# A row normalisation on one core: a second load that waits for a ScalarE write, and a last-store wait moved between two exit-barrier instructions

## The chip, the core and the metric

The kernel runs on one core of one Trainium2 chip. A core has a matrix engine (TensorE, PE, unused here), VectorE (DVE), ScalarE (ACT), GpSimd (POOL) and SyncE (SP). Each engine runs its own list of instructions in order, and semaphores order the engines against each other. Transfers between HBM and the on-chip memory are issued by an engine (here always SP) and then carried out by 16 DMA engines, which this text calls lanes. Each lane adds one to the transfer's semaphore when its share has landed, so a transfer is complete at 16.

The metric is device time in microseconds of one execution. Smaller is better.

## The reference

```python
def setup_inputs():
    batch, dim = 1024, 4096
    return {"x": np.random.randn(batch, dim).astype(np.float32),
            "axis": -1, "eps": np.float32(1e-12)}

def reference(x, axis, eps):
    norm = np.sqrt(np.sum(x ** 2, axis=axis, keepdims=True) + eps)
    return (x / norm).astype(np.float32)
```

Each of 1024 rows of 4096 float32 values is divided by its own Euclidean norm. 16.78 MB are read and 16.78 MB written.

## The kernel before

The 1024 rows are spread over 128 partitions, 8 rows to a partition, and handled in two tiles of 4 rows per partition (R = 4, n_tiles = 2). A tile is `xt`, 128 partitions by 4 x 4096 floats, 8.39 MB, and each tile has a buffer of its own. There are four transfers in all: two loads (L219) and two stores (L240), each of a whole tile, each issued by SP on its one queue. A partition's share of a tile is contiguous, 64 KB, and is one packet of a lane, so a lane moves eight packets per transfer.

For each row of a tile the work is: the sum of squares (on ACT, L33, for rows 0, 1 and 2; on DVE, L42, for row 3), the norm (ACT square root, L53, then the DVE reciprocal, L59), and the scaling in place (DVE, L64). Row 2 of the first tile is scaled by both engines, 3584 columns on ACT (L72) and 512 on DVE (L78); row 2 of the second tile is scaled on DVE alone. Then the tile is stored. The small results are `ssq` (sums of squares) and `rstd` (reciprocal norms), one column per row of the tile. `eps_t` is a 128x1 tile that DVE fills at the start (L211).

The Python program writes this down in the order of the loop at L224, but the framework's scheduler decides the order of each engine's list from what it thinks is ready. In the program as built, ACT's list in the first tile is: squares of row 0, norm of row 3, norm of row 0, squares of row 1, norm of row 1, squares of row 2, norm of row 2, scaling of row 2 (its part). In the second tile it is: squares of row 0, norm of row 0, squares of row 1, norms of rows 3 and 1, squares of row 2, norm of row 2. DVE scales in the order in which the norms come: rows 3, 0, 1, 2 in the first tile and 0, 3, 1, 2 in the second. ACT needs one table of functions for squares (loaded at the start, L33) and another for square roots (loaded before the first norm, L53).

Two functions edit the finished program by hand. `first_load_to_front` moves the first load ahead of the entry barrier, so that it is SP's first instruction; the second load follows the entry barrier. `gpsimd_waits_for_last_store` edits the end. The program ends in two barriers over the five engines. In each, the other four engines signal their arrival, GpSimd takes the four arrivals in one instruction and releases the others in the next. The function removes from SP the wait for the last store's semaphore and gives it to GpSimd: in the second exit barrier GpSimd takes the arrivals, and its releasing instruction waits for the last store (`landed`). After the release GpSimd clears the semaphores. GpSimd's own drain stands ahead of the taking.

Of the kernel before, what the change touches and what calls it, by code (L numbers as in the profile page):

```python
# [8 lines left out]
ACT_F = mybir.ActivationFunctionType  # L9
# [73 lines left out]
def first_load_to_front(nc, load):  # L83

    def move(program):  # L90
        blocks = program.main_func.blocks
        entry = blocks[0].instructions
        if any(i.name == load.name for i in entry):
            return
        body = next(
            b.instructions
            for b in blocks
            if any(i.name == load.name for i in b.instructions)
        )
        at = next(n for n, i in enumerate(body) if i.name == load.name)  # L100
        assert not body[at].sync_info.on_wait
        before = next(
            n
            for n, i in enumerate(entry)
            if i.engine == mybir.EngineType.SP and isinstance(i, mybir.InstDrain)
        )
        entry.insert(before, body.pop(at))

    nc.at_finalize(move)


def gpsimd_waits_for_last_store(nc, store):

    SP, POOL = mybir.EngineType.SP, mybir.EngineType.Pool

    def waits(i):
        return list(i.sync_info.on_wait) if i.sync_info is not None else []

    def move(program):
        sem = store.sync_info.on_update[0].id
        tail = program.main_func.blocks[-1].instructions

        def where(which):  # L130
            return [n for n, i in enumerate(tail) if which(i)]

        def semaphore(i):
            return i.engine == POOL and isinstance(i, mybir.InstEventSemaphore)

        at = where(lambda i: i.engine == SP and any(w.id == sem for w in waits(i)))
        everything = tail.pop(at[0])
        landed = [w for w in waits(everything) if w.id == sem]
        assert len(at) == 1 and len(landed) == 1
        assert not everything.sync_info.on_update  # L140
        rest = mybir.InstDrain(
            name=everything.name,
            engine=SP,
            debug=everything.debug,
            sync_info=mybir.SyncInfo(
                on_wait=[w for w in waits(everything) if w.id != sem], on_update=[]
            ),
        )
        arrival = where(lambda i: i.engine == SP and isinstance(i, mybir.InstDrain))[-1]
        tail.insert(arrival, rest)  # L150

        reset = tail.pop(
            where(
                lambda i: i.engine == POOL
                and isinstance(i, mybir.InstDrain)
                and i.is_reset_sema
            )[0]
        )
        taking, releasing = where(semaphore)[-2:]
        release = tail.pop(releasing)  # L160
        assert not waits(release)
        tail.insert(
            releasing,
            mybir.InstEventSemaphore(
                name=release.name,
                engine=POOL,
                debug=release.debug,
                sync_info=mybir.SyncInfo(
                    on_wait=landed, on_update=list(release.sync_info.on_update)
                ),  # L170
            ),
        )
        tail.insert(taking, reset)
        clear = tail.pop(
            where(lambda i: i.engine == POOL and isinstance(i, mybir.InstISA))[0]
        )
        tail.insert(1 + where(semaphore)[-1], clear)

    nc.at_finalize(move)


@with_exitstack
def kernel(
    ctx: ExitStack,
    tc: tile.TileContext,
    x: bass.AP,
    axis: bass.AP,
    eps: bass.AP,
    out: bass.AP,
):  # L190
    nc = tc.nc
    P = nc.NUM_PARTITIONS

    assert isinstance(axis, int) and axis in (-1, len(x.shape) - 1)
    eps = float(eps)

    x = x.flatten_outer_dims()
    out_flat = out.flatten_outer_dims()
    N, D = x.shape
    R = 4  # L200
    assert N % (P * R) == 0
    n_tiles = N // (P * R)
    x_t = x.rearrange("(p t r) d -> t p (r d)", t=n_tiles, r=R)
    out_t = out_flat.rearrange("(p t r) d -> t p (r d)", t=n_tiles, r=R)

    io = ctx.enter_context(tc.tile_pool(name="io", bufs=n_tiles))
    scratch_pool = ctx.enter_context(tc.tile_pool(name="scratch", bufs=1))
    stats = ctx.enter_context(tc.tile_pool(name="stats", bufs=n_tiles))

    eps_t = scratch_pool.tile([P, 1], F32)  # L210
    nc.vector.memset(eps_t, eps)  # L211
    sq_act = scratch_pool.tile([P, D], F32)
    sq_dve = scratch_pool.tile([P, D], F32)
    scratch = {"act": sq_act, "dve": sq_dve}

    groups = []
    for i in range(n_tiles):
        g = RowGroups(nc, io, stats, scratch, D, R, eps_t)
        load = nc.sync.dma_start(out=g.flat(), in_=x_t[i])  # L219
        if i == 0:  # L220
            first_load_to_front(nc, load.ins)
        groups.append(g)

    for i, g in enumerate(groups):  # L224
        g.square_dve(R - 1)
        g.square_act(0)
        g.norm(0)
        g.scale(0)
        g.square_act(1)
        g.norm(1)  # L230
        g.norm(R - 1)
        g.scale(1)
        g.scale(R - 1)
        g.square_act(2)
        g.norm(2)
        if i < n_tiles - 1:
            g.scale_by_both(2)
        else:
            g.scale(2)
        store = nc.sync.dma_start(out=out_t[i], in_=g.flat())  # L240
    gpsimd_waits_for_last_store(nc, store.ins)
# [35 lines left out]
```

## Time and profile before

| what | us |
|---|---|
| three runs | 82.04, 81.93, 81.93 (median 81.93) |
| the profiled execution's own time | 82.04 |
| its span, first to last instruction | 80.20 |
| first load issued by SP | 0.00 |
| second load issued by SP | 0.79 |
| first tile landed, squares start | 22.08 |
| first store issued by SP | 38.99 |
| second tile landed, squares start | 41.40 |
| last scaling ends, second store issued | 56.73, 56.76 |
| DVE busy, ACT busy | 26.7, 29.7 |
| DMA, busy share of its queue | 97.4% |

The span leaves out what lies around the program, 1.84 us in this execution. DVE and ACT work for a third of the span each: between 22 and 39 on the first tile and between 41 and 57 on the second. The lanes are busy nearly all the time. In the page's list of 40 slices the traffic looks like bursts, because a packet's bytes are booked in the slice in which it starts; packets of a lane follow each other all the same.

Times with two decimals come from the profile's timeline; single semaphore events and packet starts come from the trace's own records.

### The profile page before, as it was taken

Reading aid. Unit: us, or ns where it says so; the run is one execution under the profiler, and the core shown is the slowest. Engines: PE = TensorE matmul, PEld = TensorE weight load, DVE = VectorE, ACT = ScalarE, POOL = GpSimd, SP = SyncE. Lnnn points to the kernel's source line nnn. Section 1 sums busy time; section 2 is a strip of 40 time slices with the busy share of each in tenths; the row PEclk is TensorE's granted clock in tenths of the full one; section 3 lists DMA queues with packets and bytes.
Section 4 is the critical chain, followed back from the end, with each engine's and each line's share of the span. In section 5 each row is a group of like instructions: output and inputs, shape, how many; then the busy total and the mean of one; then the engine's idle time right before and its main releaser. Section 6 shows DMA issues by size and latency. Waiting matters only on the chain.

```text
span 80.2 us, 93 instructions
## 1 busy us (share of the span) xinstructions
DVE 26.7 (33%) x21; ACT 29.7 (37%) x23; POOL 0.2 (0%) x4
## 2 busy tenths in 40 slices
DVE  0000000000099599960039995999200000000000
ACT  6000000000099999989439999950000000000000
POOL 0000000000000000000000000000000000000000
DMA  9099996699996699996699990999991999992990
GB/s 490 33 523 523 523 490 294 261 523 523 523 490 261 294 523 523 523 490 261 294 523 523 523 490 33 523 523 523 523 458 65 523 523 523 523 425 98 523 523 0
DMA packets 576, 33.55 MB, mean 418 GB/s; under 512 B 64, under 2 KB 64, under 8 KB 64
## 3 DMA queue, kind: packets, MB, share of 16 engines
q1 hardware_dynamic: 576, 33.55, 97.4%
HBM read 16.78 MB, written 16.78 MB: 418 GB/s over the span
## 4 chain that ended last, share of the span: by engine, by line
DMA 51%; ACT 10%; DVE 9%; issue 0%
DMA xt<-in_x_dram 51%; ACT sq_act L33 9%; DVE xt L64 9%; ACT rstd L53 1%; DVE rstd L59 0%
## 5 line engine op out<-in xcount | busy, mean ns | idle before, releaser
L33 ACT ACTIVATE sq_act<-xt 128x4096 f32<-128x4096 f32 x6 | 21.7, 3609 | 22.4 <-DMA xt<-in_x_dram 22.4
L42 DVE SCALAR_TENSOR_TENSOR sq_dve<-xt 128x4096 f32<-128x4096 f32 x2 | 8.9, 4426 | 26.4 <-DMA xt<-in_x_dram 26.4
L64 DVE TENSOR_SCALAR xt<-xt,rstd 128x4096 f32<-128x4096 f32 x7 | 16.5, 2353 | 0.2
L72 ACT ACTIVATE xt<-xt,rstd 128x3584 f32<-128x3584 f32 x1 | 3.3, 3283 | 0.2 <-DVE rstd L59 0.2
L53 ACT ACTIVATE rstd<-ssq,eps_t 128x1 f32<-128x1 f32 x8 | 2.1, 290 | 0.1
L59 DVE RECIPROCAL rstd<-rstd 128x1 f32<-128x1 f32 x8 | 1.3, 160 | 2.5 <-ACT rstd L53 2.5
L33 ACT ACT_TABLE_LOAD x1 | 1.3, 1283 | 0.8 <-PEq L258 0.8
L53 ACT ACT_TABLE_LOAD x1 | 1.3, 1283 | 0.0
L33 ACT ACTIVATION_READ_ACCUMULATOR sq_act<-xt 128x1 f32 x6 | 1.1, 187 | 0.0
L78 DVE TENSOR_SCALAR xt<-xt,rstd 128x512 f32<-128x512 f32 x1 | 0.5, 487 | 0.0
L211 DVE MEMSET eps_t<- 128x1 f32 x1 | 0.1, 59 | 0.9 <-PEq L258 0.9
L42 DVE DVE_READ_ACCUMULATOR sq_dve<-xt 128x1 f32 x2 | 0.2, 83 | 0.0
L258 POOL MEMSET const-uint8-127<- 128x1 uint8 x1 | 0.1, 103 | 0.0
L258 POOL MEMSET const-bfloat16-1.0<- 128x1 bf16 x1 | 0.1, 102 | 0.0
L258 POOL MEMSET const-float32-0.0<- 128x1 f32 x1 | 0.1, 99 | 0.2 <-issue 0.2
L258 POOL MEMSET const-float32-1.0<- 128x1 f32 x1 | 0.1, 99 | 0.0
## 6 DMA issues: line engine op xcount, KB each, us to landing
xt<-in_x_dram SPq DMA_DIRECT2D x2, 31.3
out_dram<-xt SPq DMA_DIRECT2D x2, 22.5
```

The costliest lines, as they stand in the source:

```text
L33: self.nc.scalar.activation(out=sq_a, in_=self.x[:, r], func=ACT_F.Square, accum_out=self.ssq[:, r : r + 1],)
L42: self.nc.vector.scalar_tensor_tensor(out=sq_v, in0=self.x[:, r], scalar=1.0, in1=self.x[:, r], op0=ALU.mult, op1=ALU.mult, accum_out=self ...
L53: self.nc.scalar.activation(out=self.rstd[:, r : r + n], in_=self.ssq[:, r : r + n], func=ACT_F.Sqrt, bias=self.eps_t,)
L59: self.nc.vector.reciprocal(out=self.rstd[:, r : r + n], in_=self.rstd[:, r : r + n])
L64: self.nc.vector.tensor_scalar_mul(out=self.x[:, r], in0=self.x[:, r], scalar1=self.rstd[:, r : r + 1])
L72: self.nc.scalar.activation(out=self.x[:, r, :cut], in_=self.x[:, r, :cut], func=ACT_F.Copy, scale=rstd,)
L78: self.nc.vector.tensor_scalar_mul(out=self.x[:, r, cut:], in0=self.x[:, r, cut:], scalar1=rstd)
L211: nc.vector.memset(eps_t, eps)
L258: nc = _bacc.Bacc("TRN2", target_bir_lowering=False, num_devices=1)
```

## The change

The diff has two parts. In the first, GpSimd's instruction that takes the arrivals of the second exit barrier waits for the arrivals and for the last store, and the releasing instruction after it waits for nothing. Before, it was the other way about: the taking waited for the arrivals alone, the release for the last store.

In the second, ahead of the second tile's load, ACT writes one column of that tile's row 0 (a Square of `eps_t`, 128x1). The load overwrites the whole tile, so what is written has no part in the result. The framework orders the two writes, and the load of the second tile therefore waits on SP for ACT's semaphore.

```diff
@@ gpsimd_waits_for_last_store
-        taking, releasing = where(semaphore)[-2:]
-        release = tail.pop(releasing)
-        assert not waits(release)
-        tail.insert(
-            releasing,
-            mybir.InstEventSemaphore(
-                name=release.name,
-                engine=POOL,
-                debug=release.debug,
-                sync_info=mybir.SyncInfo(
-                    on_wait=landed, on_update=list(release.sync_info.on_update)
-                ),
+        taking = where(semaphore)[-2]
+        arrived = tail.pop(taking)
+        assert len(waits(arrived)) == 1
+        both = mybir.InstEventSemaphore(
+            name=arrived.name,
+            engine=POOL,
+            debug=arrived.debug,
+            sync_info=mybir.SyncInfo(
+                on_wait=waits(arrived) + landed,
+                on_update=list(arrived.sync_info.on_update),
             ),
         )
-        tail.insert(taking, reset)
+        tail[taking:taking] = [reset, both]
@@ tile_normalize_kernel
         g = RowGroups(nc, io, stats, scratch, D, R, eps_t)
+        if i == 1:
+
+            nc.scalar.activation(out=g.x[:, 0, 0:1], in_=eps_t, func=ACT_F.Square)
         load = nc.sync.dma_start(out=g.flat(), in_=x_t[i])
```

In the program as built from the changed source, ACT's list begins with the table load for squares, the new 128x1 write (which waits for DVE's `eps_t`), and then the squares of the first tile. The order of the first tile differs from before too: ACT's list there is now squares of row 0, norm of row 0, squares of row 1, norms of rows 3 and 1, squares of row 2, norm of row 2, scaling of row 2; DVE scales rows 0, 3, 1, 2. The second tile's order, and SP's and GpSimd's lists but for the waits named above, are as they were.

## The prediction

> **What bounds the kernel now.** I read the list of transfer issues first, then the chain of waits, then the transfers in narrow windows, then the timeline of the first tile. The issue list, page section 6:
>
> ```profile
> xt<-in_x_dram SPq DMA_DIRECT2D x2, 31.3
> out_dram<-xt SPq DMA_DIRECT2D x2, 22.5
> ```
>
> Four transfers of 8.39 MB go through one queue on the same 16 DMA engines ("lanes" below). The chain on the page gives DMA 51% and stops at the last scale, 54.38, because the two stores after it are asynchronous; so the stores must be read elsewhere. The trace's packet records show that each lane moves eight 64 KB packets per transfer. The windows below count them: GB/s times window length over 65,536 bytes is the number of packets that *start* there, and DMA share times window times 16 over that number is their mean length. Columns: window, its length, DVE, ACT and POOL busy, PE clock, DMA share, GB/s.
>
> ```profile
> 1.00:1.20 0.20, 0.00 (x0) 0.20 (x1) 0.00 (x0) 1.00 11.07 3604
> 1.45:1.55 0.10, 0.00 (x0) 0.10 (x1) 0.00 (x0) 1.00 5.27 1966
> 1.95:2.05 0.10, 0.00 (x0) 0.10 (x1) 0.00 (x0) 1.00 1.77 655
> 2.05:2.20 0.15, 0.00 (x0) 0.03 (x1) 0.00 (x0) 1.00 1.01 437
> ...
> 18.45:19.35 0.90, 0.00 (x0) 0.00 (x0) 0.00 (x0) 1.00 2.69 1165
> ...
> 40.25:40.45 0.20, 0.00 (x0) 0.00 (x0) 0.00 (x0) 1.00 0.01 0
> 40.45:40.50 0.05, 0.00 (x0) 0.00 (x0) 0.00 (x0) 1.00 6.13 2622
> 40.50:40.70 0.20, 0.00 (x0) 0.00 (x0) 0.00 (x0) 1.00 7.63 3277
> 40.70:40.80 0.10, 0.00 (x0) 0.00 (x0) 0.00 (x0) 1.00 3.03 1311
> 40.80:40.90 0.10, 0.00 (x0) 0.00 (x0) 0.00 (x0) 1.00 1.52 655
> 41.00:41.10 0.10, 0.00 (x0) 0.00 (x0) 0.00 (x0) 1.00 1.52 655
> ```
>
> What to see: a packet takes 2.42 us in steady state (18.45: 16 packets, 2.69 x 0.90 x 16 / 16), but the first ones of load 1 take 3.2 us (11 packets at 1.00). The lane that starts at 1.97 ends its first packet at 4.80, last of all, and by the records is never idle again until its last byte at 79.69. So the time is that lane: its start, then 31 packets back to back, then the landing (80.03) and the exit. At 40.25 to 41.10 load 2 hands over to store 1. Some lanes finish load 2 at 40.27 and start store 1 only at 40.49: the store was issued at 38.99, and the five lanes that were waiting for it started 1.50 to 1.69 us after that. The last lane finishes load 2 at 41.05 and goes on at once. So store 1's issue has little to spare: 41.05 - (38.99 + 1.69) = 0.37 us if the last lane's packets become ready as late as the slowest of those five, and less if later (its own readiness is only known to be under 2.06 us). What sets 38.99:
>
> ```profile
> 27.11 0.48 ACT L53 ACTIVATE rstd<-ssq,eps_t 128x1 f32<-128x1 f32 x2
> 27.50 3.60 ACT L33 ACTIVATE sq_act<-xt 128x4096 f32<-128x4096 f32 x1
> ...
> 35.68 3.28 ACT L72 ACTIVATE xt<-xt,rstd 128x3584 f32<-128x3584 f32 x1 [0.23 <-DVE rstd L59]
> 38.99 18.11 SPq L240 DMA_DIRECT2D out_dram<-xt  x2
> ...
> 45.14 0.29 ACT L53 ACTIVATE rstd<-ssq,eps_t 128x1 f32<-128x1 f32 x1
> 45.34 3.60 ACT L33 ACTIVATE sq_act<-xt 128x4096 f32<-128x4096 f32 x1
> ...
> 54.38 2.35 DVE L64 TENSOR_SCALAR xt<-xt,rstd 128x4096 f32<-128x4096 f32 x1
> ```
>
> In the first tile ACT makes two norms together at 27.11 (rows 3 and 0), so DVE has two scales ready and runs without a gap; in the second tile it makes one (45.14), and DVE idles 0.96 us until the next two.
>
> **The change, part by part.** *Load 2 issued later.* It waits for a 128x1 ACTIVATE, which waits for the table load (0.79 to 2.07, same place) and the memset of eps (done at 0.92). The row for a 128x1 ACTIVATE is 290 ns: 2.07 + 0.29 = 2.36, plus some 0.05 to reach SP, against 0.79 now: 1.6 us later. Cost taken: 0. What hides it is load 1 itself: the first lane needs load 2 at 20.94, and with 1.7 us from issue to packets there are 16.9 us of cover; uncovered it would be the whole 1.6. Behind it on SP stands only the wait for store 1, idle until 22.08; behind the small write on ACT the first squares, which wait for data until 22.08.
>
> The Trainium skill (DMA: Bandwidth & Descriptors, Rules for kernel authors) says to issue a DMA early and wait late, against this edit; by it the sum would grow by 1.6 us, which the gapless packets at 20.9 exclude here.
>
> *The first tile's order, which the diff does not show.* In the built program the extra ACT instruction makes the scheduler order tile 0 as tile 1 is: norm of row 0, squares of row 1, then the norms of rows 3 and 1. Cost from tile 1's rows: its second squares start 0.20 after its first norm (45.34 - 45.14), and its last scale starts 9.04 after those (54.38 - 45.34). For tile 0: 27.11 + 0.20 + 9.04 = 36.35, where L72 and L78 now start at 35.68. Store 1 is issued 0.67 later, at 39.66. Its packets then start at 41.16 to 41.35 (1.50 to 1.69), and the last lane, free at 41.05, stalls 0.11 to 0.30; if its packets come at the limit of 2.06, 0.67. The other lanes are free earlier and wait for the same issue; the end belongs to whichever starts last. I take 0.35: the slowest measured of five, 0.30, plus a little because the slowest of sixteen is wanted and because the packets that waited took 2.45 to 2.47 instead of 2.42. Ends: +0.11 and +0.71. What is late next: store 2 is issued at 56.76 and load 2's landing does not move, while no lane needs it before 59.79; 1.3 us of cover after 1.69 of readiness, so nothing is added there.
>
> The skill's figure (same page, Latency and other measured facts) of some 0.6 us to the first byte from SP would have store 1 ready by about 40.6 after its issue ends, before the last lane is free; by it this part would be 0. Here five lanes waited 1.50 to 1.69 from the start of an issue of 0.35, so the row is used.
>
> *The exit.* GpSimd took the arrivals at 60.9, long before, and only its release waited for the landing:
>
> ```profile
> L272 POOLq EVENT_SEMAPHORE  x4: 17/17/17, 57.3 to 80.1; - x4
> ```
>
> Now the taking waits, and the release follows it. Between taking and release in the entry and first exit barriers lie 0.08 us (0.590 to 0.668, 57.307 to 57.386, from the instruction records). Ends: 0.02 (one instruction) and 0.08; taken 0.08, uncovered, since everything after the landing is serial.
>
> *Start of load 1.* Taken 0; no row shows load 1 alone. Ends: if load 2's early issue is what slows the first packets, up to 1.19 gained (all lanes away by 1.20 with 2.42: 3.62 against 4.80); a loss of 0.01 per packet, as seen beside the issue of store 2 (2.43 at 57.3 to 58.0), at the other end.
>
> **The sum.** 0 + 0.35 + 0.08 + 0 = +0.43. The profiled execution took 82.04 (span 80.20 and 1.84 around it, unchanged): 82.47. It lies 0.11 above the median of the runs, 81.93, which gives 82.36; forecast 82.4. Its own range: +0.11 + 0.02 = 82.06 to 82.15 at the low end by the two bases, +0.71 + 0.08 = 82.7 to 82.8 at the high end.
>
> **The rivals.** *The first load gets clear* (the other side, faster). One mechanism: load 2's descriptors, following load 1's by 0.8 us, slow its first packets; moved to 2.4 they find the lanes running. For: only these first packets are slow, and load 2's issue (0.79 to 1.12) is beside them. Against: stores issued beside running packets cost 0.01; three lanes already start late at 1.48, before load 2's packets could be expected (0.79 + 1.0 as for load 1); the packet that starts at 2.12 is at the floor; the table load and a cold first access lie in the same place and stay. It decides once the last lane's first packet ends before 4.37 (4.80 - 0.43), and shows above the noise before 4.2. With packets at the floor from the same starts, 2.12 + 2.42 = 4.54, it gains 0.26 and the kernel is still slower, 82.1; fully clear, 81.93 + 0.43 - 1.19 = 81.2.
>
> *The late store is hidden anyway.* If idle lanes get their packets within 1.39 us of the issue, the last lane does not wait (39.66 + 1.39 = 41.05): +0.08, 82.0. Against: five lanes at 1.50 or more; for: load 1's came at 1.0 from idle. A small gain at the start comes to the same time.
>
> *Drained lanes restart slowly.* All 16 stall together and their first packets take 3.2 as at the start: 0.30 + 0.80 + 0.08 = 1.2, 83.1. Against: the five that waited took under 2.47, though beside eleven busy ones.
>
> *The write does not delay the load* is excluded by the built program: the load's instruction carries the wait.
>
> **Numbers.** Forecast 0.62; first load clear 0.20; hidden 0.12; slow restart 0.06. About 0.2%, 0.16 us, is what a measurement can tell from no change: faster below 81.77, slower above 82.09. Nearly all of the second case is faster, the third is the same, the others slower: 0.20, 0.12, 0.68. The range 81.4 to 82.85 holds the forecast (82.1 to 82.8), the third case and half of the second.
>
> **What would show it.** L72 starts at about 36.35 and store 1 is issued at about 39.66 if load 1 lands as before; right or wrong, 16.9 us after landing becomes 17.6. No store packet starts before 41.1, against 40.48 now, and the last at 41.3 to 41.7. Load 2 is issued near 2.4 with no gap at 20.9. GpSimd's release comes 0.1 after the landing instead of 0.05. First packets of load 1 still end at up to 4.8; if they end by 4.2 my treatment of the start is wrong, and the kernel may be faster. If store packets start under 1.4 us after their issue, the stall is wrong.

## The result, and the profile after

The changed kernel takes 82.28 us (median of six runs, 82.20 to 82.43) against 81.91 for the kernel before on the same chip: 0.37 us slower, ratio 1.0048 with a 95% interval of 1.0035 to 1.0061. The forecast was 82.4, from +0.43. The profiled execution took 82.32, its span is 80.48.

The first tile in the timeline of the changed kernel (start, length, engine, line, operation):

```profile
0.00 2.65 SPq L220 DMA_DIRECT2D xt<-in_x_dram  x2
...
2.09 0.20 ACT L219 ACTIVATE xt<-eps_t 128x1 f32<-128x1 f32 x1
```

```profile
26.98 0.29 ACT L53 ACTIVATE rstd<-ssq,eps_t 128x1 f32<-128x1 f32 x1
27.18 3.60 ACT L33 ACTIVATE sq_act<-xt 128x4096 f32<-128x4096 f32 x1
27.30 0.16 DVE L59 RECIPROCAL rstd<-rstd 128x1 f32<-128x1 f32 x1 [0.92 <-ACT rstd L53]
27.50 2.35 DVE L64 TENSOR_SCALAR xt<-xt,rstd 128x4096 f32<-128x4096 f32 x1
...
31.09 0.16 DVE L59 RECIPROCAL rstd<-rstd 128x1 f32<-128x1 f32 x1 [1.23 <-ACT rstd L53]
...
36.21 3.28 ACT L72 ACTIVATE xt<-xt,rstd 128x3584 f32<-128x3584 f32 x1 [1.03 <-DVE rstd L59]
...
39.52 0.35 SPq L241 DMA_DIRECT2D out_dram<-xt  x1
```

Two loads merged into one entry of 2.65 us show that the second now starts at 2.31, after the small write. One norm at 26.98 instead of two leaves DVE idle for 1.23 us before its second reciprocal, and the last scaling of the tile waits 1.03 us. Load 1 landed at 21.93 here and at 22.06 before, so store 1 goes out 17.59 us after the landing instead of 16.93.

The hand-over from load 2 to store 1 in narrow windows of the changed kernel (columns as in the prediction):

```profile
18.45:19.35 0.90, 0.00 (x0) 0.00 (x0) 0.00 (x0) 1.00 2.69 1165
20.90:21.65 0.75, 0.00 (x0) 0.00 (x0) 0.00 (x0) 1.00 3.24 1398
...
40.25:40.50 0.25, 0.00 (x0) 0.00 (x0) 0.00 (x0) 1.00 0.01 0
40.50:40.70 0.20, 0.00 (x0) 0.00 (x0) 0.00 (x0) 1.00 3.09 1311
40.70:40.80 0.10, 0.00 (x0) 0.00 (x0) 0.00 (x0) 1.00 4.62 1966
40.80:40.90 0.10, 0.00 (x0) 0.00 (x0) 0.00 (x0) 1.00 9.23 3932
40.90:41.00 0.10, 0.00 (x0) 0.00 (x0) 0.00 (x0) 1.00 0.01 0
41.00:41.15 0.15, 0.00 (x0) 0.00 (x0) 0.00 (x0) 1.00 3.07 1311
```

In steady state (18.45) a packet takes 2.42 us as before. From load 1 to load 2 (20.90) 16 packets start within 0.75 us as before; the later issue of load 2 is not seen. From load 2 to store 1 the counts of the four windows that hold packets, 4, 3, 6 and 3, make 16, all between 40.53 and 41.11, and they are about 2.46 us long (3.09 x 0.20 x 16 / 4 = 2.47). The packet records do not name the lane. Taken in order of time, the ends of load 2's last packets and the starts of store 1's first lie 0.19 to 0.25 us apart, 0.21 on average (the average does not depend on the pairing), and none of the 16 first packets has the 2.42 us of a lane that goes straight on. Before, 11 of 16 went straight on, with packets of 2.42.

The exit, from the same kernel's view of its last source line:

```profile
L273 POOLq EVENT_SEMAPHORE  x4: 17/17/19211, 57.2 to 80.3; - x4
```

The taking instruction now lies in wait for 19.2 us, and the release is a separate one after it. From the last landing to the release it is 0.092 us, before it was 0.024.

The two profiled executions add up like this, on the lane that ends last (an end is taken where the lane's semaphore write starts):

| part | before | after | change |
|---|---|---|---|
| its last packet of load 2 ends | 41.05 | 40.91 | -0.14 |
| pause before its first packet of store 1 | 0.01 | 0.20 | +0.20 |
| its 16 store packets | 38.63 | 38.79 | +0.15 |
| landing | 0.34 | 0.34 | 0.00 |
| landing to release | 0.02 | 0.09 | +0.07 |
| the rest: after the release, and around the program | 1.99 | 1.99 | 0.00 |
| time of that execution | 82.04 | 82.32 | +0.28 |

The -0.14 is there when load 1 lands (21.93 against 22.06), so it comes from load 1's own packets. It is scatter, as the experiments show; without it the parts come to +0.42, and the runs to +0.37.

### The profile page after: what moved, and what is told of

Its sections match the earlier page's. It is cut to its first block, busy times and chain, and to the rows that moved or that the text cites. A ratio compares the mean times of both kernels' runs of the same rounds, so it can differ in the third digit from the quotient of the medians.

```text
span 80.5 us, 94 instructions
## 1 busy us (share of the span) xinstructions
DVE 26.7 (33%) x21; ACT 29.8 (37%) x24; POOL 0.2 (0%) x4
## 4 chain that ended last, share of the span: by engine, by line
DMA 48%; ACT 12%; DVE 9%; issue 0%
DMA xt<-in_x_dram 48%; ACT sq_act L33 9%; DVE xt L64 9%; ACT L219 2%; ACT rstd L53 1%; DVE rstd L59 0%; ACT xt L219 0%
```

## The experiments

Ten kernels were run, one of them twice, each against the kernel before (medians of that one: 81.87 in the first four comparisons, 81.86 in the next four, 81.92 in the last three).

**e1: the exit edit alone.** The kernel before with the first part of the diff and without the second.

> Only the exit edit: GpSimd's taking instruction waits for arrivals and last store, the release follows; no ScalarE write. My theory: the release comes 0.07 to 0.08 us later after the landing and nothing else moves: +0.07 us, ratio about 1.001, store 1 still issued 16.9 us after load 1 lands. Rival (the exit edit carries most of the loss): +0.3 us or more, with landing to release grown by as much.

82.00, ratio 1.0016 (1.0007 to 1.0025): +0.13. In its trace the release comes 0.092 us after the landing, as in the changed kernel, and store 1 goes out 16.92 after load 1 lands. The trace accounts for 0.07; the interval in us, 0.06 to 0.20, holds it. The rival that the exit carries the loss falls.

**e2: the write alone.**

```diff
+        if i == 1:
+            nc.scalar.activation(out=g.x[:, 0, 0:1], in_=eps_t, func=ACT_F.Square)
         load = nc.sync.dma_start(out=g.flat(), in_=x_t[i])
```

> Only the ScalarE write ahead of load 2, exit as in the kernel before. My theory: the scheduler reorders tile 0 by itself, store 1 goes out 17.6 us after load 1 lands, all lanes wait for it: +0.30 us (82.2). Rival (the exit edit carries the loss): 0 or a small gain.

82.26, ratio 1.0047 (1.0033 to 1.0061): +0.39. Store 1 goes out 17.58 after the landing, the lanes pause for 0.21 on average, no first packet is shorter than 2.45, and the 16 store packets of the last lane take 38.78.

**e3 and e4: the write without its order, and the order without the write.** In e3 dependences between ACT's instructions hold tile 0 in its old order; in e4 one dependence gives the kernel before the new one.

```diff
 # e3, on top of e2, tile 0 only (follow adds an ordering edge between ScalarE instructions)
+            root = g.norm(R - 1)
+            root = g.norm(0, after=root)
+            g.scale(R - 1)
+            g.scale(0)
+            g.square_act(1, after=root)
 # e4, on top of the kernel before, tile 0 only
+            squares = g.square_act(1)
+            g.norm(R - 1, after=squares)
```

> The ScalarE write ahead of load 2 as in the last one, but tile 0's order held as in the kernel before by dependences between ScalarE instructions. My theory (the loss is the order, not the later load): store 1 again 16.9 us after load 1 lands, time within 0.1 us of before. Rival (load 2 issued 1.5 us later costs by itself): +0.3 us. Rival (load 1 gets clear of load 2 at the start): 0.14 us or more faster than before, and the first packets of load 1 near 2.4 us.

> No write and no exit edit: only tile 0's order is that of the changed kernel, held by a dependence. My theory: +0.3 to 0.45 us, as with the write (more if load 2 being later had helped the start a little), store 1 issued 17.6 us after load 1 lands, all lanes idle before it. Rival (the later load costs, not the order): within 0.1 us of before.

e3: 81.92, ratio 1.0005 (0.9996 to 1.0013), no difference that can be told. e4: 82.19, ratio 1.0045 (1.0031 to 1.0060), +0.32. This pair separates the two things that the write brings. Load 2 issued at 2.30 with the old order costs nothing; the new order with load 2 at 0.78 costs about as much as the write (+0.32 against +0.39). SP's instructions in e4 (its loads at 0.00 and 0.78 make the first entry), then those in e3 (loads at 0.00 and 2.30):

```profile
0.00 1.12 SPq L230 DMA_DIRECT2D xt<-in_x_dram  x2
39.61 17.47 SPq L260 DMA_DIRECT2D out_dram<-xt  x2
```

```profile
0.00 2.63 SPq L237 DMA_DIRECT2D xt<-in_x_dram  x2
38.78 18.11 SPq L267 DMA_DIRECT2D out_dram<-xt  x2
```

Store 1 at 39.61 is 17.59 after the landing at 22.02. In e3 it is 16.92 after the landing at 21.86, and no lane pauses at all.

**e6: store 1 late by another means.** The order stays, but ACT scales the whole of row 2 (4096 columns instead of 3584).

```diff
-        cut = 7 * self.D // 8
+        cut = self.D
 ...
-        self.nc.vector.tensor_scalar_mul(
-            out=self.x[:, r, cut:], in0=self.x[:, r, cut:], scalar1=rstd
-        )
```

> The kernel before with row 2 of tile 0 scaled on ScalarE alone, order of tile 0 untouched, so store 1 goes out some 0.43 us later (39.42). Theory of my prediction (packets are ready 1.5 to 1.7 us after the issue, a lane waits for that): store packets start at 40.92 to 41.11, pauses from 0 to 0.65 us long, the last lane hardly waits, +0.05 to +0.1 us. New theory (a pause of about 0.2 us for every lane that ends within 1.5 us of the issue, and 0.15 us more over the 16 packets that follow): the last lane goes straight on, the next ones lose 0.35, +0.15 to +0.3 us, store packets start from about 40.5. Rival (the loss belongs to the order, not to the lateness): 0.

82.06, ratio 1.0029 (1.0019 to 1.0040): +0.20. The store goes out 17.34 after the landing. Eight lanes pause for 0.20 to 0.24, eight go straight on, and packets start from 1.27 us after the issue. The rival that the loss belongs to the order and not to the lateness, with 0 here, falls, and the size fits the new account (0.15 to 0.3) rather than the prediction's (0.05 to 0.1). The lane that ended load 2 last, 1.65 us after the issue, went straight on as expected; the last to start was one that had ended at 1.53 and paused for 0.21, and from its start to the end it took 38.79.

**e8: store 1 after all lanes are empty.** On top of e6, ACT copies half of row 2 in place once more, which changes no value and only takes time.

```diff
+        half = self.D // 2
+        self.nc.scalar.activation(
+            out=self.x[:, r, :half], in_=self.x[:, r, :half], func=ACT_F.Copy
+        )
```

> As the last one, and ScalarE copies 2048 columns of that row in place once more (nothing changes in the output), so store 1 goes out at about 41.3, when all lanes are through with load 2. Measures from when a store's packets are ready. Theory of my prediction (1.5 to 1.7 us after the issue): store packets from 42.8, +1.9 to +2.3 us. New theory (ready about 0.9 to 1.0 us after the issue): from 42.2 or 42.3, +1.3 to +1.6 us. Rival (drained lanes restart as at the start of load 1, spread over 1.1 us and with first packets of 3 us): +2.4 us or more, first packets of store 1 near 3 us.

83.37, ratio 1.0183 (1.0166 to 1.0200): +1.51. The timeline and the windows of that kernel:

```profile
39.28 1.91 ACT L79 ACTIVATE xt<-xt 128x2048 f32<-128x2048 f32 x1
41.22 0.35 SPq L241 DMA_DIRECT2D out_dram<-xt  x1
```

```profile
40.10:41.90 1.80, 0.62 (x1) 1.71 (x2) 0.00 (x0) 1.00 0.01 0
42.00:42.25 0.25, 0.25 (x1) 0.25 (x1) 0.00 (x0) 1.00 9.82 4194
```

Between 40.10 and 41.90 only the 16 small semaphore writes of load 2; then all 16 store packets (4194 x 0.25 / 65.5) start between 42.00 and 42.25, by the records 42.06 to 42.21. That is 0.85 to 0.99 us after the issue. The prediction's reading that packets become ready 1.50 to 1.69 after the issue falls, and so does a restart like that of load 1: the spread is 0.14 us, and the packets are 2.46 us long (9.82 x 0.25 x 16 / 16).

**e5: store 1 early.** Row 2 of tile 0 is scaled on DVE alone.

```diff
-        if i < n_tiles - 1:
-            g.scale_by_both(2)
-        else:
-            g.scale(2)
+        g.scale(2)
```

> The kernel before with row 2 of tile 0 scaled on VectorE alone, so store 1 goes out about 0.9 us earlier (38.05). My theory now: a lane that ends load 2 more than 1.5 us after the store's issue goes straight on, one that ends sooner pauses some 0.2 us; here all 16 go straight on (ends 2.2 to 3.0 us after the issue), no lane pauses, and since the last lane did not pause before either, the time is within 0.1 us of before. Rival (the pauses of the five early lanes cost the kernel before something): 0.1 us or more faster.

82.44, ratio 1.0074 (1.0058 to 1.0089): +0.58. Both the expectation and its rival missed. All 16 lanes go straight on, as expected. The loss is ahead of that, in load 2's last packets; three windows of that kernel hold, in turn, the starts of load 2's last packets but one, of its last, and of store 1's first:

```profile
35.30:36.10 0.80, 0.74 (x2) 0.00 (x0) 0.00 (x0) 1.00 3.02 1311
37.70:38.50 0.80, 0.17 (x1) 0.00 (x0) 0.00 (x0) 1.00 3.56 1311
40.60:41.60 1.00, 0.00 (x0) 0.00 (x0) 0.00 (x0) 1.00 2.43 1049
```

Each holds 16 packets. The last load packets are 3.56 x 0.80 = 2.85 us long on average, where their neighbours are 2.42; the longest is 3.28. The store went out at 37.90, and with 0.9 us to readiness its packets stood ready at about 38.8, while those load packets (37.76 to 41.57) were under way. Load 2 lands 19.96 after load 1 (at 41.87) instead of 19.31, and everything after it is late by as much. That the waiting store stretches these packets is inferred from the times. Being ready under a load packet is not enough for it: before, by the same count, the packets of store 1 stood ready at about 39.9, and load 2's last packets, which ended as late as 41.05, still took 2.42 to 2.43.

**e11: half as early.**

```diff
-        cut = 7 * self.D // 8
+        cut = 3 * self.D // 4
```

> The kernel before with ScalarE's share of row 2 cut from 3584 to 3072 columns, so store 1 goes out 0.43 us earlier, 16.5 us after load 1 lands. Seeks the early edge, after the run with the store 0.94 us early had its last load packets stretched from 2.42 to between 2.74 and 3.28 us. If the stretch is a matter of how long the store's packets are ready before a lane's last load packet ends: a part of that loss, +0.1 to +0.4 us, last load packets between 2.45 and 2.8 us. If it is all or nothing: 0, or +0.5 us and more.

81.98, ratio 1.0005 (0.9996 to 1.0014): no difference that can be told. Store 1 goes out 16.49 after the landing. The window that holds the starts of load 2's last packets:

```profile
37.80:38.60 0.80, 0.00 (x0) 0.50 (x1) 0.00 (x0) 1.00 3.07 1311
```

Their mean is 2.46 (3.07 x 0.80 x 16 / 16). By the records 14 take 2.42 to 2.43 and two are stretched, to 2.62 and 2.72; no lane pauses. In this one execution the longer of the two is the last to end, and load 2 lands 19.49 after load 1 instead of 19.31, 0.18 late; the median of the eleven runs does not show it (the interval ends at +0.11). So the early edge begins here, it is not all or nothing, and the expected +0.1 to +0.4 is not seen in the runs.

**e10: the changed kernel with store 1 back in time.**

```diff
-        cut = 7 * self.D // 8
+        cut = 11 * self.D // 16
```

> The changed kernel with both of its edits and its order, but ScalarE's share of row 2 of tile 0 cut from 3584 to 2816 columns (VectorE takes the rest), so that store 1 goes out 16.9 to 17.0 us after load 1 lands again. My theory (the loss is when the store goes out, whatever makes it late): only the exit edit is left, +0.07 to +0.13 us against before. Rival (the order or the later load costs in another way): still +0.3 us or more.

81.94, ratio 1.0004 (0.9994 to 1.0014). SP's instructions:

```profile
0.00 2.65 SPq L220 DMA_DIRECT2D xt<-in_x_dram  x2
38.84 18.09 SPq L241 DMA_DIRECT2D out_dram<-xt  x2
```

With both edits and the new order, but store 1 out 16.95 after the landing (at 21.90), the loss is gone: no lane pauses, and the last lane's store packets take 38.63 again. The exit's 0.07 is still in the trace (0.092 from landing to release) and within the interval.

**e9 and e12: load 2 held back far.** The same kernel twice: the kernel before, with load 2 waiting for a DVE memset of half of its tile, until 9.50.

```diff
+        if i == 1:
+            nc.vector.memset(g.x[:, 0:2], 0.0)
         load = nc.sync.dma_start(out=g.flat(), in_=x_t[i])
```

> The kernel before with load 2 held back far: it waits for a VectorE memset of half of tile 1 (overwritten by the load), several us long, tile 0's order untouched. Theory (load 2's issue has no part in load 1's slow start): first packets of load 1 take 3.0 us on average as before, the last ends at 4.6 to 4.8, time within 0.1 us of before. Rival (load 2's descriptors slow load 1): first packets near 2.4 us, load 1 lands 0.3 us or more earlier, and the kernel is as much faster.

> The kernel with load 2 held back to 9.5 us once more, to tell a small gain from none (first time 0.9993, interval 0.9984 to 1.0002). My theory: no difference from before, ratio within 0.0008 of 1, first packets of load 1 at 3.0 us. Rival (load 2 out of the way at the start gains a little): 0.1 us or more faster again.

81.77, ratio 0.9993 (0.9984 to 1.0002), and 81.85, ratio 0.9990 (0.9976 to 1.0004). The first packets of load 1 in e9 (they start in the first window; the third holds the second packets):

```profile
0.95:2.00 1.05, 0.00 (x0) 1.05 (x1) 0.00 (x0) 1.00 2.87 999
2.00:3.90 1.90, 1.31 (x1) 0.07 (x1) 0.00 (x0) 1.00 0.00 0
3.90:4.80 0.90, 0.90 (x1) 0.00 (x0) 0.00 (x0) 1.00 2.69 1165
```

16 packets of 2.87 x 1.05 = 3.0 us, and none that follows before 3.9, with load 2 nowhere near. The last ends at 4.74, and load 1 lands at 21.95. So load 2 is not what makes the first packets slow. Over all thirteen profiles load 1 lands between 21.66 and 22.06, on average 21.91 in the seven with load 2 early, 21.91 in the four with it at 2.3 and 21.85 in the two with it at 9.5: scatter from one execution to the next. Both times this kernel measured 0.07 to 0.09 faster than the one before, with intervals that reach 1; whether that little is real stays open. No version here is shown to beat the kernel before.

Put in order of when store 1 goes out, counted from the landing of load 1, the runs make one curve:

| store 1 after landing | kernels | change in time |
|---|---|---|
| 15.99 | e5 | +0.58 |
| 16.49 | e11 | +0.06 |
| 16.92 to 16.95 | before; e3; e1 and e10 with the exit edit; e9 and e12 | 0; +0.05; +0.13 and +0.02; -0.09 and -0.07 |
| 17.34 | e6 | +0.20 |
| 17.58, 17.59 | e2; e4; the changed kernel with the exit edit | +0.39; +0.32; +0.37 |
| 19.29 | e8 | +1.51 |

The traces show the same curve without the scatter of load 1 and without the exit. From the landing of load 1 to that of store 2 it takes 57.95 to 57.99 us in all six traces of the middle row, 58.21 in e6, 58.28 to 58.32 in the row of the changed kernel, 59.45 in e8, and on the early side 58.18 in e11 (its two stretched packets) and 58.65 in e5. So in their traces e9 and e12 gained nothing after load 1 had landed.

## Why the prediction was right, and where it was not

**Load 2 later, cost 0.** Right: issued at 2.31 where 2.4 was written, no gap at 20.9, and e3 and e9 show no loss with load 2 at 2.30 and at 9.50.

**The first tile's order.** Right, and it is the cause. The last scaling was to start at 36.35 and the store to go out at 39.66 if load 1 landed as before; with the landing 0.13 earlier they came at 36.21 and 39.52, the 17.6 after the landing that was named. e4 shows that the order alone costs about what the write costs, e10 that it costs nothing where the store is in time.

**The stall, +0.35.** The right size by a wrong step. The prediction read the five lanes that started 1.50 to 1.69 us after the issue as waiting for packets that took so long to become ready, let no store packet start before 41.1, and had the last lane wait 0.11 to 0.30. In fact the packets are ready 0.85 to 0.99 us after the issue (e8), and store packets started from 40.53, 1.01 after the issue, the last at 41.11 and not at 41.3 to 41.7; by the prediction's own sign, a start under 1.4, this step was wrong. That the total fits is in part luck. What a lane loses is a pause of about 0.2 us whenever its last load packet ends too soon after the issue, whether 0.8 or 1.4 us after it (0.19 to 0.25 in the changed kernel, 0.20 to 0.24 in e6, 0.19 to 0.24 for the five lanes before), and then longer packets: the first 2.46, and 0.15 more over all 16. Lanes that end later than about 1.5 us after the issue nearly always go straight on at 2.42; a few did from 1.3. The pause of 0.20 and the 0.15 make the 0.35; the prediction had 0.30 for the one and allowed "a little" for the other.

The Trainium skill (DMA: Bandwidth & Descriptors, Latency and other measured facts) gives some 0.6 us to the first byte of a transfer issued by SP. e8 shows 0.50 to 0.64 us from the end of its issue of 0.35 and 0.85 to 0.99 from its start; the page does not say from where it counts, and counted from the end page and run agree. The prediction set that figure aside for the five rows, which measured something else; yet the sum drawn from it, no stall, was also wrong, since being ready in time is not enough.

**The exit, +0.08.** Right: 0.068 in the trace (0.092 against 0.024), the same in e1 and e10. e1's runs say 0.06 to 0.20.

**The start of load 1, taken as 0.** Right. The rival that load 1 gets clear has fallen with e9 and e12: first packets of 3.02 and 3.15 us on average with load 2 at 9.50. What makes them slow has not been found.

**The hidden store** as a rival had its premise fulfilled (ready within 1.39 us) and its conclusion not: lanes still pause. **The slow restart** is real but small, 2.46 instead of 3.2 for the first packet, even for lanes that were all empty.

The sum without the lucky start is 0.20 + 0.15 + 0.07 = 0.42, against 0.43 predicted and 0.37 in the runs. In the prediction's range the low end by the second basis is 82.04 + 0.13 = 82.17, not 82.15; the measured time lies above both.

## What to carry to other kernels

An extra instruction can change the built order far from where it stands; compare the built orders before costing the instruction itself, and follow the shift to the next transfer. Where the DMA engines are the bound, find for every hand-over between transfers when each lane ends the one and how long before that the next was issued; here a store behind a load was free when issued some 1.5 to 2.5 us before the lanes got to it, and neither much earlier nor later. When a sum comes out right, check its parts in the trace: a term can have the right size and stand for another process than the one it names.

## What the hardware showed that was not expected

A store issued early can cost as well as one issued late: +0.58 at 0.94 us early (e5) and +0.39 at 0.65 us late (e2). At 0.4 us either way the late one costs more, +0.20 (e6), and the early one nothing that the runs can tell (e11). The Trainium skill (DMA: Bandwidth & Descriptors, Rules for kernel authors) advises to issue a transfer early and to wait late; for this store behind a load that holds from e8 to the kernel before, each earlier issue being faster, and fails at e5, and the measurement decides. Between transfers of one direction early issue did nothing of that size: load 2 was issued 20 us ahead in the kernel before and load 1's last packets took 2.42, and store 2 is issued 2.7 to 3.9 us before the lanes reach it (4.8 to 5.0 in e8), and the last packets of store 1 take 2.42 to 2.46. Why a lane pauses although the packets are ready, why a load's last packets grow longer when the store is issued early, and why a lane that paused runs its later packets 0.01 us longer each, was not tried.
